# A last partial sum moves from the weights' ring of tiles to the operands' ring

## The chip, the cores and the metric

The kernel runs on one core of a Trainium2 chip. The metric is the time of one execution on the device in microseconds (us); lower is better. Times are medians over several executions. One further execution is recorded by the hardware profiler, and every row of a profile comes from that one.

The core has five engines that work side by side and wait for each other by semaphores: TensorE (PE in the profile) multiplies matrices, VectorE (DVE) and ScalarE (ACT) work on whole tiles, GpSimd (POOL) and SyncE (SP) do little here but issue DMA transfers. Each engine takes its instructions in its own order.

## The reference

One layer of a decoder with 2048 tokens of width 1024, in 32-bit floats. The half that matters here is the second one, a dense MLP:

```python
h = x * (1.0 + sc2) + sh2
f = jnp.square(jax.nn.relu(h @ w_mlp_in[l])) @ w_mlp_out[l]
x = _layer_norm(DEEPNORM_ALPHA * x + (1.0 + g2) * f, ln2_g[l], ln2_b[l])
```

`w_mlp_in` is 1024 x 4096, `w_mlp_out` 4096 x 1024. The first half (an input projection, a short gated convolution beside multi-scale pooling, an output projection, and a layer norm) is not touched.

## The kernel before, in words

The tokens are worked on in two blocks of 1024 (`b` = 0 and 1), and in each block the kernel runs the input projection, the output projection, the MLP's first map (`up`) and its second map (`down`). The last two work through the hidden width in eight groups of 512 columns (`NC` = 8, `g` = 0 to 7).

**Precision.** TensorE multiplies in the format float32r. Each operand is therefore split in two: a high part, which ScalarE makes by a cast (line 86), and a low part, the rest, which VectorE makes by a subtraction (line 87). `mm3` (lines 91 to 93) sums three products: high by high, high by low, low by high. So every tile that comes from memory costs one ScalarE and one VectorE instruction before TensorE can use it.

**Seven products for eight.** Every large product is done by a scheme of Strassen's kind: a 2 x 2 block product with seven multiplications, for which sums and differences of blocks are made beforehand and, where they are used twice, kept in device memory (`usum` for the squared-ReLU result, `w2sum` for the second map's weights). In the second block (`b` in `DEEPER`) one of the seven block products of `down` is itself done by seven products of quarter blocks (256 wide). These are the deep groups: `deep_matmuls` runs, for each of the eight `g`, seven products by two row tiles by three matmuls = 42 matmuls of 128x256, accumulating over `g` in seven PSUM banks. `deep_sums` then puts the seven banks together, and the ordinary steps of `down` with 128x512 matmuls follow.

**What a deep group needs.** `deep_operands(g)` (line 1209 is its load) fetches four tiles and splits each in two:

```python
for t, src, n in ((t_r, usum[g, 1], T), (lambda: t_w(F32), wdeep[g][:, :T], T),
                  (t_r, udeep[g], 3 * Q), (lambda: t_w(F32), wdeep[g][:, T:], 3 * Q)):
    r = t()
    nc.sync.dma_start(r[:, :n], src)
    hi, lo = t_h(), t_h()
    split(r[:, :n], hi[:, :n], lo[:, :n])
```

Two of the tiles are 128 x 1024 (512 KB), two 128 x 768 (384 KB). All four loads are issued on SP's queue; the stores of the kernel go by POOL's.

**The rings.** Tiles come from rings with a fixed number of slots. A tile that is asked for gets a slot only when the instructions that used that slot's last tile are done. Those that matter: `t_r` with 5 slots (what is loaded for one operand), `t_w` with 6 (weights: what is loaded for the other one, and in `up` the split weights), `t_h` with 28 (the split operands, named `h`). Tiles of all three are up to 128 x 1024. The order of the instructions on each engine is worked out when the program is built, with the rings' slots among its conditions; it isn't the order in which the Python lines stand.

**The last sum.** In `up`, each group's results are stored with their sums and differences for `down`. For the groups 0 to 6 of the second block that happens at the end of the group, in `closed`. For the last group `closed` is put in the list `left`, and `down` calls it after it has asked for the operands of the first three deep groups. `closed(s4)` (lines 1060 to 1073) writes one sum of 128 x 1024 to the tile that it is given, stores it to `usum[7, 7]`, makes the four quarter sums and stores them.

Of the kernel before, what the change touches and what calls it, by code (L numbers as in the profile page):

```python
# [8 lines left out]
F32 = mybir.dt.float32  # L9
# [39 lines left out]
def tile_hybrid_layer(ctx: ExitStack, tc: tile.TileContext, opening, xT, x, wada, win,  # L49
# [13 lines left out]
    def mk(p, shape, dt, tag, bufs):  # L63
        names[0] += 1
        return p.tile(shape, dt, name=f"{tag}_{names[0]}", tag=tag, bufs=bufs)

    def t_h(dt=F32R):
        return mk(big, [P, T], dt, "h", 28)
# [4 lines left out]
    def t_w(dt=F32R):  # L73
        return mk(big, [P, T], dt, "w", 6)
# [912 lines left out]
    left = []  # L987
# [126 lines left out]
    def down(b, F, g2, close):  # L1114
# [6 lines left out]
        def operands(n):  # L1121
            i, hf = steps[n]
            return down_operands(i, range(4 * hf, 4 * hf + 4), g2[:, lo_] if closing and n + 1 == len(steps) else None)
# [80 lines left out]
        def deep_operands(g):  # L1204
            tiles = []
# [6 lines that stand above are left out]
                tiles.append((hi, lo))  # L1212
            return tiles
# [5 lines left out]
        def deep_matmuls(banks, gs, tiles, ns):  # L1219
            for n in ns:  # L1220
                (ut, uq), (wt, wq) = DEEP[n]
                if gs[0] == 0:
                    banks.append(t_ps())
                for g in gs:
                    (uh, ul), (wh, wl) = tiles[g][ut], tiles[g][wt]
                    ws_ = slice(wq * Q, wq * Q + Q)
                    for t in range(2):
                        us = slice(uq * Q + t * P, uq * Q + t * P + P)
                        mm3(banks[n][:, t * Q : t * Q + Q], uh[:, us], ul[:, us], wh[:, ws_], wl[:, ws_],
                            g == t == 0, g == NC - 1 and t == 1, True)  # L1230

        def deep_sums(banks):
            p1, p6, p2, p7, p5, p3, p4 = banks
            def both(j, k, x, ps):
                for t in range(2):
                    src = ps[:, t * Q : t * Q + Q]
                    d = F[t + 2 * j][:, QUARTERS[k]]
                    if x is None:
                        nc.scalar.copy(d, src)
                    else:  # L1240
                        tt(d, F[t + 2 * x[0]][:, QUARTERS[x[1]]], src, ALU.add)

            both(0, 0, None, p1)
            both(0, 1, (0, 0), p6)
            both(0, 0, (0, 0), p2)
            both(1, 1, (0, 1), p7)
            both(0, 1, (0, 1), p5)
            both(0, 1, (0, 1), p3)
            both(1, 0, (1, 1), p4)
            both(1, 1, (1, 1), p5)  # L1250
# [12 lines left out]
        if deeper:  # L1263
            tiles = {}
            for g in range(3):
                tiles[g] = deep_operands(g)
            left.pop()(t_w(F32))
            banks = []
            for gs, ns in (((g,), range(7)) for g in range(NC)):
                for g in gs:  # L1270
                    if g + 3 < NC and g + 3 not in tiles:
                        tiles[g + 3] = deep_operands(g + 3)
                if gs[-1] == NC - 1:
                    ready = operands(2)
                deep_matmuls(banks, gs, tiles, ns)
            deep_sums(banks)
        else:
            ready = operands(0)
# [116 lines left out]
    def mlp(b, B, back, g2):  # L1395
# [25 lines left out]
        if b == 0:  # L1421
            g2 = mk(sm, [P, D], F32, "bc", 1)
        close = Close(b, F)
        down(b, F, g2, close)
        if close.late:
            close.finish(*close.late)
# [62 lines left out]
```

## Time and profile before

| | us |
|---|---|
| median of 3 executions | 1737.52 |
| lowest, highest | 1736.49, 1739.21 |
| the profiled execution, its own time | 1738.77 |
| its span in the profile | 1737.0 |

| engine | busy us | share of the span |
|---|---|---|
| TensorE, matmuls | 1725.7 | 99% |
| TensorE, weight loads (beside the matmuls) | 1436.7 | 83% |
| VectorE | 1313.2 | 76% |
| ScalarE | 867.8 | 50% |
| GpSimd | 205.7 | 12% |

The profile's times count from the start of the span. A timeline row gives start, duration, engine, line of the kernel, operation, the tile written and the tiles read (`h<-w` is a split operand made from a tile of the weights' ring), the shape, and in square brackets how long the engine had been idle before it and what ended that. SPq is SP's queue of transfers: a row there is the issue of a transfer, not the transfer. Rows with a count merge neighbours of the same kind. The granted clock is the share of TensorE's full clock that the chip allowed in a stretch. The DMA share is the mean busy share of the core's 16 DMA engines.

### The profile page before, as it was taken

The page shows a single profiled execution, that of the slowest core. Times are in us where ns is not written, and L with a number is a line of the kernel's source. Part 1 is how long each engine was busy: PE and PEld are TensorE (multiplying, and loading weights), DVE is VectorE, ACT ScalarE, POOL GpSimd, SP SyncE. Part 2 cuts the span into 40 slices and gives each one's busy share as a digit, 9 for nine tenths or more (in the row PEclk, how much of TensorE's full clock was granted, in tenths as well). Part 3 has the DMA queues.
Part 4 walks back from the last instruction along what each step waited for, and adds up shares of the span by engine and source line. Part 5 has one row for each costly group of instructions (what it writes and reads, how often), then busy time and mean ns, then how long its engine had stood idle before and what let it go on. Part 6 is the DMA issues. An engine that isn't in the chain of part 4 may idle for free.

```text
span 1737.0 us, 21910 instructions
## 1 busy us (share of the span) xinstructions
PE 1725.7 (99%) x7855; PEld 1436.7 (83%) x7855; DVE 1313.2 (76%) x1726; ACT 867.8 (50%) x1172; POOL 205.7 (12%) x399
## 2 busy tenths in 40 slices
PE   9999999999999999999999999999999999999998
PEld 7888888888888888888888888888888889888887
DVE  8897798877777676759687789697666758665896
ACT  6323368554454654436573345765455567444451
POOL 0222220122322000100000000101111100000000
PEclk9999999999999999999999999999999999999999
DMA  9998777778888998887572266657545579876771
GB/s 388 344 335 323 300 267 267 263 269 320 312 333 322 385 418 320 316 296 262 187 259 91 92 227 221 226 200 284 193 176 221 224 259 402 308 277 248 266 264 50
DMA packets 142685, 465.24 MB, mean 268 GB/s; under 512 B 16488, under 2 KB 17008, under 8 KB 142576
## 3 DMA queue, kind: packets, MB, share of 16 engines
q1 hardware_dynamic: 97920, 303.39, 47.8%
q0 software_dynamic: 44656, 160.46, 24.3%
q8 instruction: 61, 1.00, 0.2%
q14 instruction: 48, 0.39, 0.1%
HBM read 318.55 MB, written 145.23 MB: 267 GB/s over the span
## 4 chain that ended last, share of the span: by engine, by line
PE 99%; DMA 1%; DVE 0%; SPq 0%; issue 0%; ACT 0%; DVEq 0%
PE ps L93 32%; PE ps L91 32%; PE ps L92 32%; PE ps L423 3%; PE ps L771 1%; DMA w<-wdeep 0%; DMA o<-in_opening 0%; DVE o L1359 0%; SPq L106 0%; PE ps L147 0%; ACT h L86 0%; DVE o L1365 0%; DVEq L1485 0%; DVE h L394 0%; DVE tmp L1334 0%
## 5 line engine op out<-in xcount | busy, mean ns | idle before, releaser
L93 PE MATMUL ps<-h,w 128*128 128x512 f32 x1312 | 510.4, 389 | 0.0
L92 PE MATMUL ps<-h,w 128*128 128x512 f32 x1312 | 510.3, 389 | 0.0
L91 PE MATMUL ps<-h,w 128*128 128x512 f32 x1312 | 510.0, 389 | 0.0
L91 PE MATMUL ps<-h,h 128*128 128x512 f32 (+1 forms) x1176 | 444.5, 379 | 1.9 <-ACT h L86 1.8
L92 PE MATMUL ps<-h,h 128*128 128x512 f32 (+1 forms) x1176 | 444.3, 378 | 0.0
L93 PE MATMUL ps<-h,h 128*128 128x512 f32 (+1 forms) x1176 | 444.3, 378 | 0.0
L86 ACT CAST h<-r 128x1024 fp32r<-128x1024 f32 (+1 forms) x192 | 193.4, 1011 | 296.5 <-PE ps L92 182.9
L87 DVE TENSOR_TENSOR h<-r,h 128x1024 fp32r<-128x1024 f32 (+1 forms) x192 | 223.5, 1169 | 93.7 <-ACT h L86 93.3
L93 PEld LDWEIGHTS ps<-h,w 128*128 128x128 f32 x1312 | 246.3, 188 | 51.7 <-DVE w L87 0.7
L92 PEld LDWEIGHTS ps<-h,w 128*128 128x128 f32 x1312 | 246.2, 188 | 51.7 <-DVE h L87 0.5
L86 ACT CAST w<-r 128x1024 fp32r<-128x1024 f32 x156 | 164.2, 1053 | 249.1 <-PE ps L92 241.0
L91 PEld LDWEIGHTS ps<-h,w 128*128 128x128 f32 x1312 | 246.0, 188 | 51.4 <-ACT h L86 0.2
L87 DVE TENSOR_TENSOR w<-r,w 128x1024 fp32r<-128x1024 f32 x156 | 190.3, 1221 | 104.5 <-ACT w L86 103.8
L91 PEld LDWEIGHTS ps<-h,h 128*128 128x128 f32 x1176 | 221.6, 189 | 43.2 <-ACT h L86 2.5
L92 PEld LDWEIGHTS ps<-h,h 128*128 128x128 f32 x1176 | 221.7, 189 | 41.0
L93 PEld LDWEIGHTS ps<-h,h 128*128 128x128 f32 x1176 | 221.7, 189 | 40.7
L96 DVE TENSOR_TENSOR o<-o,o 128x1024 f32<-128x1024 f32 (+2 forms) x193 | 170.8, 889 | 40.4 <-DMA usum<-o 33.7
L96 DVE TENSOR_TENSOR o<-o,ps 128x512 f32<-128x512 f32 (+1 forms) x175 | 113.6, 657 | 55.1 <-PE ps L93 54.2
L87 DVE TENSOR_TENSOR h<-w,h 128x1024 fp32r<-128x1024 f32 x120 | 143.9, 1199 | 8.7 <-ACT h L86 8.5
L86 ACT CAST h<-w 128x1024 fp32r<-128x1024 f32 x120 | 124.2, 1035 | 20.2 <-DMA w<-wdeep 11.1
L1011 POOL DMA_DIRECT2D usum<-o x111 | 59.4, 535 | 473.9 <-ACT o L1008 188.4
L96 DVE TENSOR_TENSOR r<-r,r 128x1024 f32<-128x1024 f32 x60 | 73.3, 1222 | 20.0 <-DMA r<-in_w 16.4
(158 smaller groups left out, 1218.1 us busy)
## 6 DMA issues: line engine op xcount, KB each, us to landing
r<-usum SPq DMA_DIRECT2D x112, 512.0 KB, 5.5
usum<-o POOLq DMA_DIRECT2D x111, 512.0 KB, 4.9
w<-w2sum SPq DMA_DIRECT2D x64, 512.0 KB, 6.2
r<-in_w SPq DMA_DIRECT2D x60, 512.0 KB, 6.0
w<-in_w SPq DMA_DIRECT2D x40, 512.0 KB, 7.0
o<-in_w SPq DMA_DIRECT2D x72, 256.0 KB, 6.3
w2sum<-o POOLq DMA_DIRECT2D x64, 256.0 KB, 6.8
msum<-o POOLq DMA_DIRECT2D x18, 512.0 KB, 4.3
```

Of the source, the lines that this page charges most:

```text
L86: high = nc.scalar.copy(hi, src)
L87: return high.ins, nc.vector.tensor_tensor(lo, src, hi.bitcast(F32), op=ALU.subtract).ins
L91: nc.tensor.matmul(ps, whi, xhi, start=first, stop=False, skip_group_check=goes_on)
L92: nc.tensor.matmul(ps, whi, xlo, start=False, stop=False, skip_group_check=goes_on)
L93: nc.tensor.matmul(ps, wlo, xhi, start=False, stop=last, skip_group_check=goes_on)
L96: return nc.vector.tensor_tensor(out_, a, b_, op=op)
L423: nc.tensor.matmul(ps[m, h], wt[:, w : w + P], A[k][p // 2][:, hs], start=k == 0 and p == 0, stop=k == KD - 1 and p == 2)
L771: nc.tensor.transpose(ps[:, t * P : t * P + P], R[4 * h + t][:, k * P : k * P + P], ident)
L1011: nc.gpsimd.dma_start(usum[g, i], r)
```

## The change

The tile for the last sum is taken from the ring of the split operands (`t_h`, 28 slots) and not from the ring of the weights (`t_w`, 6 slots). Shape, type, values and the store are the same.

```diff
@@ -1264,7 +1264,7 @@
             tiles = {}
             for g in range(3):
                 tiles[g] = deep_operands(g)
-            left.pop()(t_w(F32))
+            left.pop()(t_h(F32))
             banks = []
             for gs, ns in (((g,), range(7)) for g in range(NC)):
                 for g in gs:
```

## The prediction

> **What bounds the kernel now.** I read the page first (busy shares, then the chain that ended last), then TensorE's and SP's waits, and then the timeline of each engine around the one long wait of TensorE.
>
> ```profile
> PE 1725.7 (99%) x7855; PEld 1436.7 (83%) x7855; DVE 1313.2 (76%) x1726; ACT 867.8 (50%) x1172; POOL 205.7 (12%) x399
> PE 99%; DMA 1%; DVE 0%; SPq 0%; issue 0%; ACT 0%; DVEq 0%
> PE ps L91 <- ACT h L86: 1.8, 1, 1.8
> SPq L1209 <- DMA usum<-w: 6.0, 1, 6.0
> ```
>
> TensorE is busy for 1725.7 of 1737.0 us, so no edit that leaves its matmuls alone can win more than 11.3 us. Its longest wait (third line: total, times, longest) is one of 1.8 us on a cast of line 86. It lies in the stage that the change touches. TensorE's timeline there (start, duration, instruction):
>
> ```profile
> 1423.90 0.28 PE L91 MATMUL ps<-h,h 128*128 128x256 f32 x1
> ...
> 1440.99 1.53 PE L91 MATMUL ps<-h,h 128*128 128x256 f32 x4 [1.81 <-ACT h L86]
> ...
> 1463.08 0.28 PE L91 MATMUL ps<-h,h 128*128 128x256 f32 x1
> ...
> 1468.12 0.40 PE L91 MATMUL ps<-h,h 128*128 128x512 f32 x1
> ```
>
> The eight deep groups of the second block start at 1423.90; the next step starts at 1468.12. Group 7, the last, takes from 1463.08 to 1468.12, 5.04 us for its 42 matmuls (7 products, 2 row tiles, 3 each), so 0.12 us a matmul. Eight such groups would end at 1423.90 + 40.32 = 1464.22. The stage loses 3.9 us: 1.81 in the wait ahead of group 3, which begins when group 2 is done at about 1439.1, and the rest behind it. The windows say why (columns: stretch, length, busy time of PE, PEld, DVE, ACT and POOL, granted clock, DMA share, GB/s):
>
> ```profile
> 1437.84:1441.25 3.41, 1.60 (x14) 1.40 (x12) 0.28 (x1) 1.36 (x2) 0.58 (x2) 1.00 0.93 315
> 1441.25:1444.66 3.41, 3.27 (x15) 2.95 (x15) 3.41 (x4) 2.31 (x4) 0.00 (x0) 0.50 1.04 422
> ...
> 1727.97:1731.39 3.42, 1.76 (x15) 1.56 (x14) 2.80 (x7) 0.29 (x1) 0.00 (x0) 1.00 0.38 153
> 1731.39:1734.80 3.41, 0.00 (x0) 0.00 (x0) 2.55 (x6) 0.88 (x3) 0.00 (x0) 1.00 0.17 61
> ...
> 1447.96:1453.00 5.04, 5.04 (x45) 5.04 (x44) 5.04 (x6) 4.80 (x6) 0.00 (x0) 1.00 1.03 419
> ```
>
> A stretch with TensorE busy for 1.60 of 3.41 us (47%) is followed by 3.41 us at half clock. At the close, one with 1.76 (51%) is followed by full clock. In this trace the switch lies between the two. The last row shows the stage's other limit: the DMA engines are full (share 1.03) at 419 GB/s.
>
> **Why group 3 waits.** I call group g's loads Ug (usum, 512 KB), Wg (first part of wdeep, 512 KB), ug (udeep, 384 KB) and wg (rest of wdeep, 384 KB). First SP's queue, then the casts:
>
> ```profile
> 1422.42 0.32 SPq L1209 DMA_DIRECT2D r<-udeep  x1
> 1426.42 0.32 SPq L1209 DMA_DIRECT2D r<-usum  x1
> 1430.70 0.32 SPq L1209 DMA_DIRECT2D r<-udeep  x1
> 1432.70 0.32 SPq L1209 DMA_DIRECT2D r<-usum  x1
> 1433.12 3.29 SPq L1209 DMA_DIRECT2D w<-wdeep  x5
> 1436.51 0.50 SPq L1209 DMA_DIRECT2D r<-udeep  x1
> 1443.14 0.32 SPq L1209 DMA_DIRECT2D w<-wdeep  x1
> ```
>
> ```profile
> 1439.89 1.04 ACT L86 CAST h<-w 128x1024 fp32r<-128x1024 f32 x1 [8.11 <-DMA w<-wdeep]
> 1440.84 0.83 ACT L86 CAST h<-r 128x768 fp32r<-128x768 f32 x1
> 1442.06 0.83 ACT L86 CAST h<-w 128x768 fp32r<-128x768 f32 x1 [0.39 <-DMA w<-wdeep]
> ...
> 1444.55 1.05 ACT L86 CAST h<-w 128x1024 fp32r<-128x1024 f32 x1 [0.72 <-DMA w<-wdeep]
> ...
> 1447.04 0.83 ACT L86 CAST h<-w 128x768 fp32r<-128x768 f32 x1 [0.70 <-DMA w<-wdeep]
> ```
>
> In the order of the built program, SP issues behind U3: u3, U4, u4, U5 (the first four rows), then W3, w3, W4, w4, W5 (the five from 1433.12), u5, and w5 at 1443.14. The last sum takes one of the weights' ring's six slots between group 2's loads and group 3's, so W3 comes after it, and stands in the queue behind loads of groups 4 and 5. ScalarE idles for 8.11 us and starts W3's cast at 1439.89, 0.8 us after TensorE has run dry.
>
> **The change, part by part.** No instruction is added or dropped: the sum keeps operands and size, its store its 512 KB and its place on POOL's queue.
>
> The weights' ring. In the changed program SP issues behind U3: W3, u3, w3, U4, W4, u4, w4, U5, W5, u5, w5. W3 and w3 get the slots of the two parts of the last product, whose matmuls end where the deep groups begin. SP so waits for TensorE until about 1424 and then issues W3, not at 1433.12. Behind this new wait stands u3 (issued at 1422.42 before) and all that follows; U3 and loads of group 2 are still moving then, so the DMA engines don't run dry, and ScalarE and VectorE, who need u3 after 1439, don't notice. w5 no longer waits for the sum's store (the 6.0 us in the SP row of waits; the store lands when w5 is issued, at 1443.1).
>
> The operands' ring. The sum takes one of 28 slots, so each of the next 28 tiles takes over a tile freed a little later, in the built program that of a group three or more before its own: no wait while TensorE is less than two groups late. The sum's own slot goes to W5's low part, which then waits for the store of 1443.1, and is made only after 1449 (below). Cost nothing; if the store came 7 us later, it would cost what it is late.
>
> TensorE's order within groups 3 and 4 becomes the plain one, product by product. SP's order farther on differs in a few neighbouring loads of the residual, where TensorE's list of waits has no entry: nothing.
>
> What is late next. The DMA engines are full, so W3 only changes places: what has landed by a given time stays the same. I count units of 128 KB behind U3. Before, W3 completed 18 units (cast at 1439.89), w3 21 (1442.06), W4 25 (1444.55), w4 28 (1447.04). At 419 GB/s 512 KB take 1.25 us and 384 KB 0.94, so W5 completed 32 at 1448.3, u5 35 at 1449.2, w5 38 at 1450.2. In the new order w3 completes 10, well before 1439.9; W4 18 at 1439.9; u4 21 at 1442.1; w4 24 at 1443.9 (between two rows); U5 28 at 1447.0; W5, u5 and w5 as before. Each then needs its cast (1.05 or 0.83 us) and VectorE's low part:
>
> ```profile
> 1436.74 0.41 DVE L96 TENSOR_TENSOR o<-o,o 128x256 f32<-128x256 f32 x1
> 1440.97 1.23 DVE L87 TENSOR_TENSOR h<-w,h 128x1024 fp32r<-128x1024 f32 x1 [3.81 <-ACT h L86]
> ...
> 1451.13 0.95 DVE L87 TENSOR_TENSOR h<-r,h 128x768 fp32r<-128x768 f32 x1
> 1452.00 0.95 DVE L87 TENSOR_TENSOR h<-w,h 128x768 fp32r<-128x768 f32 x1
> ...
> 1460.02 0.95 DVE L87 TENSOR_TENSOR h<-w,h 128x768 fp32r<-128x768 f32 x1
> ```
>
> VectorE's idle 3.81 us fill up: the low parts of W3, u3 and w3 are ready at 1438.3, 1439.2 and 1440.0 (W3's was at 1442.2). TensorE uses w's low part with the eighth matmul, 0.84 us into a group, and then has 35 matmuls, 4.2 us, to go. Group 3 starts at 1439.0, idles 0.15 us for w3 and ends at 1444.2. w4's cast ends at 1444.75, its low part at 1445.75, wanted at 1445.05: 0.7 idle, group 4 ends at 1449.95. W5's low part is there at 1450.55, wanted at 1450.05: 0.5 idle. w5's is there at 1452.3 (before: at 1452.95, the row at 1452.00), wanted at 1451.3: 1.0 idle, and group 5 ends at 1456.5. Groups 6 and 7 stay behind their low parts (the last, the row at 1460.02, is there by 1461; group 7 wants it at 1462.4) and end at 1466.6.
>
> Sum: 1468.12 - 1466.6 = 1.5 us, of 3.9 lost. The rest isn't removed but moved, from one long wait with a half-clock stretch behind it into small waits of groups 4 and 5. Against the profiled execution's own 1738.77 us that gives 1737.2. It lies 1.25 us above the median, 1737.52. Whether the old wait falls into one 3.41 us stretch and so halves the clock may differ by run; without that, the old order still ends no sooner than w5's low part allows, 1452.95 + 4.2 + 2 x 5.04 = 1467.2, and 0.6 is gained. Between 0.6 and 1.5 I take 1.2 against the median: 1736.3.
>
> The Trainium skill bears on two terms. "DMA: Bandwidth & Descriptors", Specifications, puts a core's limit to HBM at some 358 GB/s; by it W5, u5 and w5 would take 0.5 us longer behind 1447.0 and the gain would be an estimated 1.0 us. The 419 GB/s row disagrees and decides. "TensorE: Matmul & The Clock Gate", Part 1: The HAM clock gate, has the clock fall to half after an idle window of some 3.4 us; by it the second rival below could not occur. The row with 1.60 busy of 3.41 disagrees: half an idle window was enough here.
>
> **The rivals.** First, all is won back: 3.9 us, 1733.6. For it: only 315 GB/s were moved around 1439, so a smoother queue might land w4, W5 and w5 the microsecond sooner that this needs. Against it: the share was 0.93 even there, so little is unused. Chance 0.17.
>
> Second, slower: the new waits halve the clock. My count has at most 1.5 us idle in one stretch of 3.41; from 1.7 on (half) the clock falls and costs half a stretch, 1.7 us. It decides if the loads of groups 4 and 5 land 0.4 us later than counted: the stage then ends at 1466.6 + 0.4 + 1.7 = 1468.7, 0.6 later than before, 1738.1. Chance 0.15.
>
> Third, landing times don't follow the order of issue, and the change does nothing: 1737.5. Against it, the four waiting casts above follow SP's order. Chance 0.10.
>
> Fourth, a wait behind the stage: in the new order VectorE makes the low parts of the next step's second pair of loads ahead of the additions that free the banks of that step. Were a load some 8 us late, TensorE would wait there, some 4 us net: 1741.5. Nothing shows such a load. Chance 0.05.
>
> **How the numbers follow.** The forecast, 1736.3, has 0.53. Measurements of this kernel tell about 0.2%, 3.5 us, from no change. Faster by more: the first rival and 0.03 of the forecast's, by the runs' spread (1736.49 to 1739.21): 0.20. Slower by more: the fourth and 0.03 of the second's: 0.08. Within: 0.72. The range runs from the first rival, 1733.6, past the second to 1738.8 by that spread.
>
> **What would show it.** Right: the wait of 1.8 us gone; wdeep's loads issued one by one between the others; W3's cast near 1432; short waits in groups 4 and 5; no half-clock stretch; the 128x512 step 1.5 us sooner, and all behind it shifted alike. Wrong: groups 3 to 7 back to back (first rival), a half-clock stretch (second), W3's cast still behind 1439 (third), a wait behind 1466 (fourth).

## The result and the profile after

The changed kernel takes 1734.96 us (median of 22 executions, 1734.32 to 1736.43); the kernel before, run beside it, 1737.75 (22 executions, 1736.49 to 1740.19). The ratio is 0.9983, 95% interval 0.9977 to 0.9990: 2.8 us less. Forecast were 1736.3 and a gain of 1.2. The profiled execution took 1735.93 us where that of before took 1738.77.

The page and TensorE's list of waits (total, times, longest) of the changed kernel:

```profile
PE 1724.6 (99%) x7855; PEld 1436.3 (83%) x7855; DVE 1313.6 (76%) x1726; ACT 868.4 (50%) x1172; POOL 205.0 (12%) x399
```

```profile
PE ps L125 <- DVE o L127: 1.1, 1, 1.1
PE ps L92 <- DVE h L87: 0.8, 1, 0.8
PE ps L423 <- DVE h L394: 0.2, 1, 0.2
```

The wait of 1.8 us on a cast of line 86 is gone. A new one of 0.8 stands in line 92, on a low part. TensorE's timeline places it, and gives the stage's two ends:

```profile
1423.34 0.28 PE L91 MATMUL ps<-h,h 128*128 128x256 f32 x1
...
1448.76 0.28 PE L91 MATMUL ps<-h,h 128*128 128x256 f32 x1
1449.16 0.38 PE L92 MATMUL ps<-h,h 128*128 128x256 f32 x1
...
1449.86 0.28 PE L91 MATMUL ps<-h,h 128*128 128x256 f32 x1
1450.90 0.39 PE L92 MATMUL ps<-h,h 128*128 128x256 f32 x1 [0.76 <-DVE h L87]
...
1465.27 0.40 PE L91 MATMUL ps<-h,h 128*128 128x512 f32 x1
```

The deep groups take from 1423.34 to 1465.27, 41.93 us, where they took 44.22. That is 2.3 of the 2.8 us between the two spans (1737.0 and 1734.2). Another 0.56 is that the stage starts earlier in this profile (1423.34 for 1423.90), and that is chance: over all the profiles below it starts anywhere from 1422.97 to 1425.42. From the stage's end to the span's end nothing moved: 268.9 us in both. Inside the stage, group 5 begins at 1448.76, where it waits some 0.3 us for W5's low part and 0.9 for w5's.

The windows of both kernels, with the columns of the prediction's windows. First the changed kernel: the whole stage, two stretches of 5.04 us from its first half, and the old stretch of the wait. Then the kernel before: its whole stage and the same two stretches.

```profile
1423.34:1465.27 41.93, 41.05 (x338) 40.47 (x336) 38.13 (x42) 31.04 (x38) 3.20 (x6) 1.00 1.02 403
1428.94:1433.98 5.04, 5.04 (x44) 5.04 (x43) 5.04 (x6) 4.59 (x6) 0.53 (x1) 1.00 1.01 401
1433.98:1439.02 5.04, 5.04 (x44) 5.04 (x43) 5.04 (x9) 2.52 (x3) 1.60 (x3) 1.00 1.03 418
1437.84:1441.25 3.41, 3.41 (x29) 3.25 (x28) 3.41 (x4) 2.24 (x3) 0.00 (x0) 1.00 1.03 422
```

```profile
1423.90:1468.12 44.22, 42.27 (x338) 41.74 (x337) 38.23 (x42) 31.00 (x38) 3.21 (x6) 0.96 1.01 388
1428.94:1433.98 5.04, 5.04 (x45) 5.04 (x44) 5.04 (x6) 2.84 (x4) 0.53 (x1) 1.00 0.94 353
1433.98:1439.02 5.04, 5.04 (x44) 4.99 (x42) 3.18 (x6) 0.00 (x0) 1.61 (x3) 1.00 0.98 322
```

Two things are to be seen. The mean granted clock of the stage goes from 0.96 to 1.00: no half-clock stretch is left. And the last column: between 1428.94 and 1439.02 the DMA engines moved 401 and 418 GB/s where they had moved 353 and 322, at a share of 1.01 and 1.03 against 0.94 and 0.98. That is (401 + 418 - 353 - 322) x 5.04 = 0.73 MB more in ten microseconds. The prediction had counted on none. These rates hold loads and stores together; the account of the prediction below tells them apart.

SP's queue and ScalarE's casts of the changed kernel:

```profile
1423.31 0.32 SPq L1209 DMA_DIRECT2D w<-wdeep  x1
1423.72 0.92 SPq L1209 DMA_DIRECT2D r<-udeep  x1
1424.73 0.39 SPq L1209 DMA_DIRECT2D w<-wdeep  x1
1425.75 0.32 SPq L1209 DMA_DIRECT2D r<-usum  x1
1426.12 0.48 SPq L1209 DMA_DIRECT2D w<-wdeep  x1
```

```profile
1431.00 1.06 ACT L86 CAST h<-w 128x1024 fp32r<-128x1024 f32 x1
...
1440.51 0.84 ACT L86 CAST h<-w 128x768 fp32r<-128x768 f32 x1 [1.17 <-DMA w<-wdeep]
1444.01 1.05 ACT L86 CAST h<-r 128x1024 fp32r<-128x1024 f32 x1 [2.66 <-DMA r<-usum]
1446.80 1.05 ACT L86 CAST h<-w 128x1024 fp32r<-128x1024 f32 x1 [1.74 <-DMA w<-wdeep]
...
1448.62 0.83 ACT L86 CAST h<-w 128x768 fp32r<-128x768 f32 x1
```

SP issues W3, u3, w3, U4 and W4 one after the other from 1423.31; W3 had gone out at 1433.12. The casts shown are those of W3, w4, U5, W5 and w5.

### The profile page after: what moved, and what is told of

The parts are those of the page before. It is cut to its first block, busy times and chain, and to the rows that moved or that the text cites. A ratio compares the mean times of both kernels' runs of the same rounds, so it can differ in the third digit from the quotient of the medians.

```text
span 1734.2 us, 21910 instructions
## 1 busy us (share of the span) xinstructions
PE 1724.6 (99%) x7855; PEld 1436.3 (83%) x7855; DVE 1313.6 (76%) x1726; ACT 868.4 (50%) x1172; POOL 205.0 (12%) x399
## 4 chain that ended last, share of the span: by engine, by line
PE 97%; DMA 1%; DVE 1%; issue 0%; ACT 0%; DVEq 0%; SPq 0%; ACTq 0%
PE ps L92 31%; PE ps L91 31%; PE ps L93 31%; PE ps L423 3%; DMA w<-wdeep 1%; PE ps L771 1%; DVE h L87 0%; PE ps L147 0%; DVE h L198 0%; PE ps L125 0%; ACT h L86 0%; DVE o L96 0%; DVE o L1359 0%; DVE o L1365 0%; DVEq L1485 0%
```

## The experiments

Most effects here are smaller than what varies between executions, so each kernel is read in two ways: by its median against the kernel before on the same chip, and by the length of its deep stage in its profile, from the first matmul of 128x256 to the first of 128x512 behind it. Without a loss the stage takes 40.32 us.

| kernel | stage, us | median, us | ratio to before (95%) |
|---|---|---|---|
| before | 44.22 | 1737.75 | |
| before, again | 45.05 | (one execution, 1740.55) | |
| change | 41.93 | 1734.96 | 0.9983 (0.9977 to 0.9990) |
| change, again | 41.41 | 1734.95 | 0.9980 (0.9971 to 0.9989) |
| change, third | 40.69 | 1735.02 | 0.9979 (0.9970 to 0.9988) |
| weights' ring, behind group 3 | 41.05 | 1734.75 | 0.9978 (0.9969 to 0.9987) |
| ring of ten | 40.93 | 1735.76 | 0.9981 (0.9972 to 0.9990) |
| before + 15 matmuls | 45.98 | 1739.61 | 1.0005 (0.9996 to 1.0014) |
| before + 30 matmuls | 44.35 | 1738.34 | 1.0002 (0.9993 to 1.0011) |
| change, three stores fewer | 40.50 | 1735.80 | 0.9983 (0.9974 to 0.9992) |
| operands' ring, behind group 3 | 40.31 | 1734.87 | 0.9980 (0.9972 to 0.9989) |
| the same, again | 40.32 | 1735.53 | 0.9982 (0.9973 to 0.9991) |
| operands' ring, behind group 4 | 42.70 | 1736.86 | 0.9990 (0.9982 to 0.9999) |

The kernel before had medians of 1738.67, 1738.33 and 1738.64 beside the three sets of experiments.

**Is it the tile or the place in the queue?** The sum stays in the weights' ring and is taken one group later:

```diff
-            left.pop()(t_w(F32))
             banks = []
             for gs, ns in (((g,), range(7)) for g in range(NC)):
                 for g in gs:
                     if g + 3 < NC and g + 3 not in tiles:
                         tiles[g + 3] = deep_operands(g + 3)
+                if left:
+                    left.pop()(t_w(F32))
```

> The kernel before, but the last sum keeps its tile of the weights' ring and takes it one group later, behind group 3's loads. If the gain of the change is that W3 and w3 are no longer issued behind u3, U4, u4 and U5 (the place in SP's queue), then W3 lands near 1428.6 us as with the change, TensorE's 1.81 us wait ahead of group 3 and the half-clock stretch go, and the held-back weights are now W4, issued near 1432.5 behind u4 and U5: a smaller wait (0.3 to 1.5 us) ahead of group 4, and 1735.2 to 1736.5 us. If instead it is the tile itself that costs (a weights' slot kept until the sum's store has landed, so that one load fewer can be in flight), the time stays at the kernel before's 1737.5 +- 0.5 with the wait merely moved to group 4.

SP's queue, and TensorE's one wait in the stage:

```profile
1423.32 0.32 SPq L1209 DMA_DIRECT2D w<-wdeep  x1
...
1430.43 0.32 SPq L1209 DMA_DIRECT2D r<-udeep  x1
1432.44 0.32 SPq L1209 DMA_DIRECT2D r<-usum  x1
1432.81 1.44 SPq L1209 DMA_DIRECT2D w<-wdeep  x3
```

```profile
1444.99 0.39 PE L92 MATMUL ps<-h,h 128*128 128x256 f32 x1 [0.49 <-DVE h L87]
```

W3 is issued at 1423.32, and the late block of three weights' loads, W4, w4 and W5, now goes out from 1432.81. Group 4 loses 0.74 us in all, half an idle microsecond among it, and the kernel takes 1734.75 us, a little under the 1735.2 to 1736.5 expected and level with the change. So the tile in the weights' ring is not by itself what cost: its place was, ahead of the loads of the group that was needed next. The same late block, one group later, costs 0.7 us in place of nearly four, since TensorE has a group more in hand.

**Another ring.** The changed line with `t_o()` in place of `t_h(F32)`:

```diff
-            left.pop()(t_h(F32))
+            left.pop()(t_o())
```

> The changed kernel with the sum in a tile of the ring of ten (t_o) in place of the split operands' ring. If only leaving the weights' ring matters, it equals the changed kernel: 1735.0 us, within 0.5, with the same three small waits of TensorE in the stage. If taking a slot of the operands' ring costs something by itself (a later operand that waits for the sum's store), this one is faster by up to 1 us.

The stage took 40.93 us, inside the change's own three (40.69 to 41.93). The ratio to before is 0.9981, the change's 0.9979 to 0.9983. Its median, 1735.76, is 0.8 above what was expected, but its profile lost 1.9 us between 446 and 561 us, far from the stage (the stretch from TensorE's 2000th matmul to the 2500th took 115.3 us, 113.3 in the change). The kernel without three stores lost 1.7 there, the others at most 0.4. How many of the executions behind the median lost it isn't known. In the stage no cost or gain of the ring chosen in place of the weights' ring can be seen.

**The half clock.** Two kernels fill TensorE's wait in the kernel before with matmuls whose result is not used, 15 in one and 30 in the other:

```diff
+                if gs[0] == 2:
+                    fill = t_ps()
+                    (uh, _), (wh, _) = tiles[2][0], tiles[2][1]
+                    for _ in range(15):
+                        nc.tensor.matmul(fill[:, :Q], uh[:, :P], wh[:, :Q], start=True, stop=True)
```

> The kernel before with 15 more matmuls of 128x256 (0.12 us each, 1.8 us) behind deep group 2, into a free bank, their result not used: TensorE is busy while it waits for W3. The late W3 and all loads stay as before. If the half-clock stretch is most of what the change wins, this kernel wins most of it too: 1735.2 to 1736.0 us. If the change wins by loads that come earlier (w5 at 1448.5 and not 1450.0), only the part that the half clock cost beyond the late loads is won: the stage then ends with group 5 held by w5, at 1467.2 or later for 1468.1, so 1736.6 to 1737.3 us.

> The kernel before with 30 matmuls of 128x256 behind deep group 2 whose result is not used (3.6 us at 0.12), where the run with 15 still showed 1.6 us of waits and the half clock. If the half clock comes from TensorE's waits, both are gone: the stage is 40.32 + 3.6 = 43.9 to 44.2 us, some 2 us less than with 15 such matmuls (45.98) though twice the work is added, and the time is that of the kernel before within 0.5 us. What the late loads alone cost is then 3.4 to 3.6 us of the 3.9, and the half clock at most 0.5. If the half clock does not hang on the waits, it stays and the stage takes 46 us or more, 1739.5 and over.

With 15, neither of the two expected answers came. The stage became longer, 45.98 us, and nothing was won: the median is 0.9 above that of the kernel before, which is within the noise (1.0005, 0.9996 to 1.0014). TensorE's waits behind the fill, then the whole stage and the stretches ahead of the slow clock and in it:

```profile
1441.16 0.39 PE L92 MATMUL ps<-h,h 128*128 128x256 f32 x1 [0.88 <-DVE h L87]
1443.10 0.58 PE L92 MATMUL ps<-h,h 128*128 128x256 f32 x1 [0.61 <-DVE h L87]
```

```profile
1422.97:1468.95 45.98, 44.41 (x353) 43.75 (x351) 39.56 (x43) 32.22 (x39) 3.20 (x6) 0.96 1.01 388
1439.43:1442.84 3.41, 2.10 (x13) 1.44 (x11) 2.85 (x3) 2.77 (x4) 0.00 (x0) 1.00 1.03 412
1442.84:1446.25 3.41, 3.15 (x14) 3.15 (x15) 2.85 (x4) 2.55 (x4) 0.00 (x0) 0.51 1.02 417
```

The fill took the wait on W3's cast, but TensorE still idled for 0.88 and 0.61 us ahead of W3's and w3's low parts, and the clock fell as before. This run could not tell the clock from the loads. The one with 30 could:

```profile
1438.39 3.76 PE L1280 MATMUL ps<-h,h 128*128 128x256 f32 x30
...
1443.18 0.39 PE L92 MATMUL ps<-h,h 128*128 128x256 f32 x1 [0.19 <-DVE h L87]
```

```profile
1423.28:1467.63 44.35, 44.16 (x368) 43.95 (x366) 39.64 (x43) 32.17 (x39) 3.20 (x6) 1.00 1.00 389
1437.00:1440.41 3.41, 3.41 (x30) 3.41 (x30) 0.33 (x1) 1.41 (x2) 0.79 (x2) 1.00 0.92 309
```

With twice the added work the stage is 1.6 us shorter, and the clock is 1.00 throughout. In this stage the waits bring the half clock on; filled with enough work, they don't. The loads are as slow as ever (309 GB/s in the second row). From the stage's start to group 4's first matmul, worked out from the starts of all matmuls, it takes 25.82 us with 15, 24.19 with 30, and 24.06 and 24.89 in the two profiles of before. In all four w3's low part is the last operand that group 3 gets, and w3 came at slightly different times: its cast starts 18.25, 18.03, 18.16 and 18.58 us behind the stage's start. So of the 1.6 us between the two fills some 1.4 are the half clock, which came behind the waits with 15. In the kernel before it cost next to nothing in one profile; in the other, 0.55 of the 0.7 us above the run with 30 are w3's own lateness. There much of the half clock ran while w3's low part wasn't there yet. The late loads are nearly the whole loss.

**What is left in group 5.** Three of the last group's stores in `up` (sums 4, 6 and 5) are left out of the changed kernel:

```diff
-        for i, r in ((4, s1), (6, c12), (5, c11)):
+        for i, r in ((4, s1), (6, c12), (5, c11)) if b == 0 or g + 1 < NC else ():
             save(r, i)
```

> The changed kernel without three of the stores of the second block's last group (sums 4, 6 and 5, 1.5 MB that stand in the DMA queues between the deep loads; the output lacks them). If what is left of the waits ahead of deep group 5 (about 1.3 us) is bytes that the DMA engines cannot move sooner, W5 and w5 land some microseconds earlier, those waits go, and the time is 1.0 to 1.6 us under the changed kernel, 1733.4 to 1734.0. If the loads are issued too late, one by one as slots come free, whatever the stores do, the waits stay and the time is that of the changed kernel within 0.4 us.

> The changed kernel once more, for a second profile of the stage. The eight deep groups took 44.21 us before and 41.92 with the change, and what follows them took 261.34 us in every profile so far. If the stage is fixed by the order of its DMAs, it takes 41.9 +- 0.3 us again with the wait of about 1.4 us in group 5 in the same place. If the DMA engines' sharing moves from run to run, the wait changes its size or its group, and the stage lies anywhere between 40.9 and 42.5 us.

> The changed kernel a third time, beside the one with the sum behind group 3's loads on the same chip, for the comparison and for a third profile of the stage: 41.92 and 41.41 us so far. If group 5's wait is there each time, 40.9 to 42 us, with the wait in group 5; a stage under 40.7 would say that the wait is chance.

The whole stage without the stores, and one stretch of it, then the whole stage in the second and third profiles of the change:

```profile
1425.42:1465.92 40.50, 40.50 (x337) 40.36 (x336) 39.81 (x44) 32.54 (x40) 1.61 (x3) 1.00 1.02 395
1433.98:1439.02 5.04, 5.04 (x44) 5.04 (x44) 5.04 (x9) 5.04 (x8) 0.83 (x2) 1.00 1.00 350
```

```profile
1423.07:1464.48 41.41, 40.82 (x338) 40.42 (x336) 37.95 (x41) 31.03 (x38) 3.20 (x6) 1.00 1.01 401
```

```profile
1423.77:1464.46 40.69, 40.56 (x337) 40.35 (x336) 38.07 (x41) 31.11 (x38) 3.20 (x6) 1.00 1.02 406
```

Without the stores group 5 doesn't wait, but the median, 1735.80, is 0.8 us above the change's, which fits neither expected answer. In the third profile of the change itself group 5 doesn't wait either: it lost 1.39, 0.81 and 0 us in the three, and w5 landed at 1448.5, 1448.0 and 1447.9 by the transfers' own records. The wait is real and small, and differs from execution to execution, so one profile without the stores proves nothing about them. This question stays open; it is worth half a microsecond or so.

**The kernel before again.**

> The kernel before once more, for a second profile of the stage: 44.2 us in the first. If the wait ahead of group 3 and the half clock behind it come from the order of the loads, both stand at the same place and the stage takes 43.9 to 44.5 us. If the half clock is chance, it is absent, and the stage takes 43.7 us or less.

TensorE's wait, and the whole stage with the stretch of the slow clock:

```profile
1442.34 0.50 PE L91 MATMUL ps<-h,h 128*128 128x256 f32 x2 [2.23 <-ACT h L86]
```

```profile
1424.84:1469.89 45.05, 42.57 (x337) 41.95 (x336) 38.62 (x42) 31.33 (x38) 3.20 (x6) 0.96 1.01 387
1444.06:1447.47 3.41, 3.41 (x19) 3.41 (x18) 2.87 (x4) 2.69 (x4) 0.00 (x0) 0.51 1.04 425
```

Wait and half clock stand in the same place, as expected of the order of the loads; the stage is 0.8 us longer than in the first profile, above the 43.9 to 44.5 expected. Its mean over two profiles is 44.6 us, the change's over three 41.3: 3.3 us, and the three comparisons of the medians give 2.8, 3.4 and 3.6. As far as two and three profiles tell, the stage holds the whole gain.

**A version that should be better.** The sum in the operands' ring and taken later, behind group 3's loads, or behind group 4's:

```diff
-            left.pop()(t_h(F32))
...
                         tiles[g + 3] = deep_operands(g + 3)
+                if left:                 # behind group 4's: if left and g == 1
+                    left.pop()(t_h(F32))
```

> The changed kernel (sum in the split operands' ring), with the sum also taken one group later, behind group 3's loads, as in the run where it stayed in the weights' ring. There group 4 lost 0.74 us by W4, issued behind u4 and U5, and group 5 nothing, since the stores of the last sums came behind w5. With the other ring W4 follows U4 again: if both things hold, group 4's loss goes and group 5's stays away, the stage takes 40.4 to 40.7 us (41.92 with the change) and the time is about 1.2 us under the changed kernel, 1733.7 where it has 1734.9. If the two stores merely push another load, a wait of 0.5 to 1.4 us shows in group 4 or 5 and the time equals the change's.

> As the run with the sum in the split operands' ring behind group 3's loads, but behind group 4's. The stores of the last sums are then issued behind group 6's loads of the weights. If what is left of the waits is those stores among the deep loads, no wait over 0.3 us is left in the stage, which takes 40.4 to 40.6 us, 1.4 under the change: about 1733.5. Its risk: the last group's first load waits for its store, and lies then at the end of SP's queue; if that store lands behind 1456 us a wait opens ahead of group 7 and the time is back at 1735 or over.

> The kernel with the sum in the split operands' ring behind group 3's loads once more, beside the changed kernel on the same chip. In its first profile the deep stage had no wait left (40.31 us, 41.41 and 41.92 with the change), but its median was only 0.08 us under the change's. If the profile stands for the runs, it is 0.8 to 1.4 us under the change here. If the change's own stage loses less in most runs than in its two profiles, or other parts take the gain back, it is 0 to 0.5 us under it and cannot be told from it.

Behind group 3's loads the stage has no loss at all, in both profiles (40.31 and 40.32 us), and still the kernel isn't faster: 1734.87 beside the change's 1734.95 on one chip, 1735.53 beside 1735.02 on the other, where it was expected below. Part of it is seen behind the stage. In the second profile 269.9 us follow it, not 268.9 (span 1734.1, stage's end 1464.22), in the first 269.2:

```profile
1469.22 0.50 PE L91 MATMUL ps<-h,h 128*128 128x512 f32 x1 [0.73 <-DVE o L96]
```

```profile
1465.48 0.75 DVE L96 TENSOR_TENSOR o<-o,ps 128x256 f32<-128x256 f32 x2
...
1468.74 0.42 DVE L96 TENSOR_TENSOR o<-o,ps 128x256 f32<-128x256 f32 x1
```

TensorE waits there for a PSUM bank, which VectorE frees by the additions of `deep_sums`; these stand on VectorE behind low parts of the next step's operands and begin 1.26 us after the stage's end (1465.48; 1463.96 in the third profile of the change, with the stage's end at 1464.46). That is 0.2 and 1.0 us given back in the two profiles. The rest of what the 0.4 to 1.6 us in the stage should have brought to the medians isn't traced.

Behind group 4's loads, the risk that the expectation names came, and earlier than it said. SP's, ScalarE's and TensorE's rows in that kernel:

```profile
1453.13 0.32 SPq L1209 DMA_DIRECT2D r<-usum  x1
```

```profile
1457.07 1.05 ACT L86 CAST h<-r 128x1024 fp32r<-128x1024 f32 x1 [5.72 <-DMA r<-usum]
```

```profile
1460.56 0.39 PE L92 MATMUL ps<-h,h 128*128 128x256 f32 x1 [1.07 <-DVE h L87]
...
1462.30 0.39 PE L92 MATMUL ps<-h,h 128*128 128x256 f32 x1 [0.76 <-DVE h L87]
```

Group 7's first load waits for the store of the last group's result. It is issued at 1453.13, so that store had landed by then, not behind 1456; but the tile is cast only at 1457.07, and group 7 loses 2.4 us. No version beat the change by more than can be measured.

## Why the prediction was right, and where it was too small

**The wait and its cause: right.** W3's load stood behind those of groups 4 and 5. With either kernel that issues it at 1423, its wait is gone. The prediction has the cast "near 1432"; it is at 1431.00.

**The loss of 3.9 us: the sum right, the parts less so.** A second profile gave 4.7. The prediction gave 1.81 us to the wait and put the rest down to the half clock behind it. The run with 30 matmuls shows that at a full clock the loads alone hold group 3 as long as in the first profile of before: the rest is mostly w3's low part.

**"The DMA engines are full, so W3 only changes places": wrong, and the step that failed.** The prediction took the share of 0.93 for an engine with little unused, and so let the loads that had landed by any time stay the same. They did not. By casts: w4 was counted on to land at 1443.9 and was cast at 1440.51; U5 1447.0 and 1444.01; W5 1448.3 and 1446.80; w5 1450.2 and 1448.62. The whole queue was 1.5 to 3.4 us ahead of the count, 0.56 us of it because this execution reached the stage sooner. So the later loads were not late by what W3 was early; they came earlier too. Here is what SP's queue (loads) and POOL's queue (stores) moved in the first 15 us of the stage, each counted from its own profile's start of the stage:

| profile | first 10 us: loads, MB | stores, MB | both, GB/s | next 5 us: loads, MB | stores, MB | both, GB/s |
|---|---|---|---|---|---|---|
| before | 1.97 | 1.50 | 348 | 1.54 | 0.08 | 324 |
| before, again | 1.95 | 1.44 | 341 | 1.50 | 0.14 | 328 |
| change | 2.75 | 0.83 | 358 | 1.28 | 0.81 | 417 |
| change, again | 2.68 | 0.80 | 350 | 1.28 | 0.82 | 419 |
| change, third | 2.90 | 0.82 | 371 | 1.30 | 0.79 | 418 |

In the first ten microseconds the engines move hardly more than before, but with W3, w3 and W4 in the queue early it is 0.7 to 0.95 MB more of loads and 0.6 to 0.7 MB less of stores. In the next five the stores catch up at a higher rate, and the loads keep a lead of 0.45 to 0.74 MB, over a microsecond at 419 GB/s. The prediction's count had the loads alone in it, and no stores that could give way.

Why the rate was low in the kernel before is not shown. In the first ten microseconds SP stood on waits for slots of the ring `t_r` with few loads behind it in flight. But that does not explain the 324 GB/s behind them, where the six loads issued from 1433.12 to 1437.01 were on their way; nor does the lack of stores, since the same profile moves loads alone at 419 GB/s from 1447.96 to 1453.00. The run without three stores moved 350 GB/s at a share of 1.00 in the stretch from 1433.98: a full share doesn't mean a full rate.

**The new waits: the place right, the size too large.** Forecast were 0.15 us in group 3, 0.7 in group 4 and 1.5 in group 5. Three profiles gave 0.22, 0.29 and 0.38; none at all; and 1.39, 0.81 and 0. Group 4's hung on w4's landing, so it fell with the count above; group 5's was as forecast in the first profile and less in the others.

**The sum.** A stage of 42.7 us was forecast (1423.90 to 1466.6), and 41.93, 41.41 and 40.69 came. Between 0.6 and 1.5 us of gain the forecast took 1.2, with 0.6 for executions in which the old wait doesn't halve the clock. Both profiles of before have the half clock, and the gain was larger than either end. The measured 1734.96 lies about as far from the forecast, 1736.3, as from the first rival, 1733.6. The range from 1733.6 to 1738.8 held both, and no change too, so that the time fell into it says little for the count of landings; the direction and the wait that went say more.

**The rivals.** All won back: not in the first profile, nearly in the third (40.69 of 40.32), so it was underrated; its reason, a smoother queue, is the one that held. The half clock by the new waits: in none of three. Nothing changed: no. A wait behind the stage: not with this change, but with the sum behind group 3's loads, at 0.2 to 1.0 us, and by the order on VectorE that the prediction names. In its second profile no load was late there: the cast ahead of the low part had waited 1.37 us for TensorE.

**The two rules of the Trainium skill** that were weighed against the trace fared as in the trace of before. "DMA: Bandwidth & Descriptors", Specifications, puts the limit at some 358 GB/s, as half of a memory stack's 716 for two cores; the change, a program on one core, ran at 401 to 422 for more than ten microseconds. "TensorE: Matmul & The Clock Gate", Part 1: The HAM clock gate, asks for an idle window of some 3.4 us; the run with 15 matmuls halved the clock after a stretch of 3.41 us that the busy column shows idle for only 1.3.

## What to carry to other kernels

A tile for a side job, taken from the same ring as a stream of loads, holds back every load that comes after it in the program, and what is issued instead fills the queue ahead of it: ask which load gets a slot later, how far it falls back in the issue order, and how soon TensorE needs it. Read the GB/s beside the DMA share before calling the transfers a limit, and read loads and stores apart: a load issued earlier can take the place of a store that isn't needed yet, and not only of another load. And when one stage has been cleared, look at the stage behind it and at several profiles, since a microsecond won in one trace may be chance or be given back 5 us later.

## What the hardware showed that was not expected

The DMA engines' busy share says little about their rate: shares from 0.94 to 1.03 stood beside 322 to 422 GB/s in this one stage, before and after, and a share of 1.00 beside 350.

The granted clock followed less than the busy column suggests. In the run with 15 matmuls it halved after a stretch of 3.41 us in which TensorE is shown busy for 2.10 (62%), though at the close of the kernel before, after 1.76 (51%), it had not, nor after 1.88 and 1.97 at the close of the runs without three stores and with the sum behind group 3's loads. The number of matmuls puts them in order: 14 in the stretch ahead of the half clock in the kernel before, 13 with 15 filling ones, but 15, 16 and 17 in the three closes. At 0.12 us each the 13 are 1.6 us of work, 46%. The profile gives a lone matmul 0.28 to 0.39 us, and the sum of such rows counts too much where matmuls stand apart. That the clock goes by the work itself is read from these five stretches, not tested. In the three profiles that show the slow clock in this stage, one stretch of 3.41 us holds nearly all of it (0.50 to 0.51 in its row).
